# Projecting the convolution groups first and evacuating two tiles at once, in a one-core decoder trunk

## The chip, the cores and the metric

The kernel runs on one core of a Trainium2 chip. The metric is the device time of one execution in microseconds (us), the median over several runs. The kernel before takes 1127.89 us (three runs, 1125.96 to 1129.59).

The core's engines have names in the profile: PE is TensorE (matrix products), DVE is VectorE, ACT is ScalarE, POOL is GpSimd, SP is SyncE, which here only issues DMAs. Each engine works off its own queue of instructions in order. SBUF is the on-chip memory, PSUM the memory in which products are accumulated, in banks of 512 float32 columns.

## The reference, cut to what matters

One layer of a decoder on 256 prompt tokens and 8 x 4 sample tokens, 288 columns in all, in float32:

```python
h = rmsnorm(x, norm1_g)
proj = h @ w_in + b_in                      # 2048 -> 3072
a, gate, z = proj[:1024], proj[1024:2048], proj[2048:]
u = a * sigmoid(gate)
c = silu(layernorm(depthwise_causal_conv(concat(hist_conv, u), conv_w, conv_b)))   # 31 taps
d = window_mean(concat(hist_pool, z)) - z   # four groups of 256 channels, windows 2, 4, 8, 16
p = (d per group @ pool_w) * pool_scale
x = x + concat(c, p) @ w_out
f = square(relu(rmsnorm(x, norm2_g) @ w_ff1))   # 2048 -> 8192
x = x + f @ w_ff2
y = rmsnorm(x, norm_f)
```

The last 30 columns of `u` and the last 15 of `z` are returned too, as new states.

## The kernel before, in words

Activations lie with the channel on the partitions and the 288 tokens along the columns, one tile for 128 channels. Every float32 operand of a large product is split into a high and a low part, and a product is three matrix instructions: high x high, high x low, low x high (lines 233 to 235). Weights come in blocks of 1 MB by SP's DMAs (`load`, three buffers). `split` makes four half-parts of each pair of blocks: ACT copies out the high part (`whi`, line 213), and DVE or GpSimd subtracts it to get the low part (`wlo`, line 214). The table `SHARE` says how many of eight low parts go to GpSimd: 7 in a convolution group, 5 in a pooling group, 6 in the output projection's pooling half, none from there on. There are four buffers for high and four for low parts, so a group's parts are made while the group before is multiplied.

A group of products (`gemm`) fills two PSUM banks, m = 0 and 1, with 128 channels each; four banks (`acc`) let one group be read out while the next is multiplied.

The stages:

- Start: x is loaded in pieces, scaled and split (`hh`, `hl`), squares are summed in two chains, and `rsqrt_rows` makes the token's 1/rms, which later scales the projection's result as `rb`. `rsqrt_rows` uses small products (`pt`, line 182), a few tiny DVE operations (`st`), a diagonal (`dg`) and one more product (`pr`, line 196).
- Input projection: twelve groups of 96 products in the order of `SEQUENCE`. A `conv` group gives tile i of `a` and of `gate`: DVE reads both banks (`tg`, `ta`, lines 302 and 303), ACT applies the sigmoid, DVE makes `u` in `u_all` (line 308), and the convolution of that tile follows: for the prompt 31 taps on DVE, the first a `tensor_scalar` into PSUM (line 313), 29 more accumulating in PSUM and the last into `c` (line 316); for the samples four multiplications on GpSimd (`prd`) and a reduction on DVE (line 321). The convolution stands under `later()`, which gives it a low priority: the scheduler puts it where DVE has room. GpSimd sums the tiles `c` into `sum_c`. A `pool` group gives the two tiles of one pooling group. For each tile DVE reads the bank (`tz`, line 341), ACT adds the bias into `z_all`, GpSimd makes window sums by doubling (`s`, line 347: four additions for window 16, one for window 2), DVE makes `d` (line 351), its sample columns (line 354) and its first w - 1 columns (`e` and `d`, lines 358 and 359), ACT and DVE split it (`dh`, `dl`, line 362).
- Pool products: four groups of 12 products, g = 3, 2, 1, 0, scaled and split (`ph`, `pl`, line 380).
- LayerNorm of `c`: a product with ones gives the mean (`pmean`), DVE subtracts it (line 390), ACT squares, DVE adds up (`ssc`, line 397), `rsqrt_rows`, then scale, SiLU and split (`mh`, `ml`).
- Output projection: eight groups of 48 products over the pooling half, eight over the convolution half, each added to `xT`.
- MLP in four chunks of 2048: eight groups of 96 products up, eight down, with ReLU, square and split between.
- The last group of the last chunk is ordered with all of m = 0 first (`m_outer`), then the final RMSNorm.

The order of the instructions on each engine is made by a scheduler at build time, from the program's order, the priorities and its own estimate of durations. On the chip each queue is then strictly in order, with waits on the other engines' counters. The two state outputs have the lowest priority; SP's queue holds them among the weight loads.

## Time and profile before

| | |
|---|---|
| median of 3 runs | 1127.89 us |
| lowest, highest run | 1125.96, 1129.59 us |
| profiled execution: span from first to last instruction | 1125.9 us (the page gives no time around it) |
| PE busy | 1094.4 us, 97% |
| DVE busy | 677.1 us, 60% |
| ACT busy | 468.7 us, 42% |
| POOL busy | 188.8 us, 17% |
| data moved by DMA | 187 MB, 166 GB/s on the mean |

How to read it: busy times are sums over the span, so they hide stages with different limits. The page also shows the span in 40 slices, with each engine's busy tenths and PE's granted clock. Views of the trace give the same for any stretch (busy time and number of instructions of each engine, clock, DMA share), groups of instructions by line with their mean duration and the idle time before them, the waits by pair of engines, the chain of waits that ended last, and the instructions in order of time. Tile names stand as output<-inputs, buffer numbers left out.

### The profile page before, as it was taken

How to read it: one execution, taken by the hardware profiler on the slowest of the kernel's cores; microseconds unless marked ns; L12 is line 12 of the kernel's file. 1: busy time of each engine (PE TensorE's matmuls, PEld its weight loads, DVE VectorE, ACT ScalarE, POOL GpSimd, SP SyncE). 2: the span in 40 equal slices, each digit the busy share in tenths (PEclk: the TensorE clock that was granted, in tenths of full speed). 3: DMA queues.
4: the chain of work that ended last, by engine and by line, in shares of the span. 5: the costliest groups of instructions: out<-in, count | busy, mean ns of one | idle time of the engine just before them, and what ended most of it. 6: DMA issues, size and time to landing. Idle time of an engine off the chain costs nothing.

```text
span 1125.9 us, 19336 instructions
## 1 busy us (share of the span) xinstructions
PE 1094.4 (97%) x8190; PEld 1089.8 (97%) x8190; DVE 677.1 (60%) x983; ACT 468.7 (42%) x643; POOL 188.8 (17%) x149
## 2 busy tenths in 40 slices
PE   7998898999999999999999999999999999999995
PEld 7998898999999999999999999999999999999995
DVE  7999999788755544445555444455444445555554
ACT  6443345356544433334444333344433334444441
POOL 4789886612200000000000000000000000000000
PEclk9999998989999999999999999999999999999998
DMA  8554438534445444444445454444444454545432
GB/s 298 191 175 164 148 115 222 184 113 166 172 150 177 160 171 167 158 179 154 184 153 183 152 182 156 174 163 167 170 160 178 153 184 151 183 155 175 162 113 84
DMA packets 31910, 187.01 MB, mean 166 GB/s; under 512 B 3408, under 2 KB 7760, under 8 KB 10448
## 3 DMA queue, kind: packets, MB, share of 16 engines
q1 hardware_dynamic: 31824, 185.78, 47.0%
q8 instruction: 64, 1.05, 0.4%
q14 instruction: 22, 0.18, 0.0%
HBM read 181.49 MB, written 4.28 MB: 165 GB/s over the span
## 4 chain that ended last, share of the span: by engine, by line
PE 86%; DVE 9%; POOL 2%; issue 2%; DMA 1%; ACT 0%; SPq 0%; DVEq 0%; POOLq 0%
PE ac L233 29%; PE ac L234 28%; PE ac L235 28%; DVE pc L316 3%; DVE wlo L214 1%; POOL wlo L214 1%; DVE d L354 1%; DVE ssc L397 1%; DVE d L351 1%; DMA xT<-in_xT 1%; POOL s L347 0%; DVE d L359 0%; DVE z_all L283 0%; PE pt L182 0%; DVE xT L481 0%
## 5 line engine op out<-in xcount | busy, mean ns | idle before, releaser
L213 ACT CAST whi<-wr 128x1024 fp32r<-128x1024 f32 (+1 forms) x342 | 355.0, 1040 | 562.8 <-PE ac L234 543.6
L214 DVE TENSOR_TENSOR wlo<-wr,whi 128x1024 fp32r<-128x1024 f32 (+1 forms) x295 | 364.7, 1236 | 371.8 <-ACT whi L213 371.7
L233 PE MATMUL ac<-ah,whi 128*128 128x288 f32 x1024 | 302.7, 296 | 0.0
L233 PE MATMUL ac<-fh,whi 128*128 128x288 f32 x1024 | 302.4, 295 | 0.0
L234 PE MATMUL ac<-al,whi 128*128 128x288 f32 x1024 | 301.2, 294 | 0.0
L234 PE MATMUL ac<-fl,whi 128*128 128x288 f32 x1024 | 301.2, 294 | 0.0
L235 PE MATMUL ac<-fh,wlo 128*128 128x288 f32 x1024 | 299.3, 292 | 0.0
L235 PE MATMUL ac<-ah,wlo 128*128 128x288 f32 x1024 | 298.8, 292 | 0.0
L235 PEld LDWEIGHTS ac<-fh,wlo 128*128 128x128 f32 x1024 | 193.1, 189 | 0.0
L235 PEld LDWEIGHTS ac<-ah,wlo 128*128 128x128 f32 x1024 | 192.9, 188 | 0.0
L234 PEld LDWEIGHTS ac<-fl,whi 128*128 128x128 f32 x1024 | 192.7, 188 | 0.0
L234 PEld LDWEIGHTS ac<-al,whi 128*128 128x128 f32 x1024 | 192.4, 188 | 0.1
L233 PEld LDWEIGHTS ac<-ah,whi 128*128 128x128 f32 x1024 | 192.1, 188 | 0.1
L233 PEld LDWEIGHTS ac<-fh,whi 128*128 128x128 f32 x1024 | 192.0, 188 | 0.0
L233 PE MATMUL ac<-hh,whi 128*128 128x288 f32 x384 | 113.6, 301 | 7.7 <-DVE tg L302 6.6
L214 POOL TENSOR_TENSOR wlo<-wr,whi 128x1024 fp32r<-128x1024 f32 (+1 forms) x47 | 112.3, 2400 | 34.0 <-ACT whi L213 31.4
L234 PE MATMUL ac<-hl,whi 128*128 128x288 f32 x384 | 114.9, 301 | 3.0 <-DVE hl L246 2.9
L235 PE MATMUL ac<-hh,wlo 128*128 128x288 f32 x384 | 114.2, 301 | 1.5 <-DVE wlo L214 1.4
L316 DVE SCALAR_TENSOR_TENSOR pc<-u_all,vec,pc 128x256 f32<-128x256 f32 x232 | 100.1, 479 | 1.3
L233 PEld LDWEIGHTS ac<-hh,whi 128*128 128x128 f32 x384 | 73.3, 193 | 8.4 <-issue 7.0
L234 PEld LDWEIGHTS ac<-hl,whi 128*128 128x128 f32 x384 | 74.3, 194 | 4.1 <-DVE hl L246 4.1
L235 PEld LDWEIGHTS ac<-hh,wlo 128*128 128x128 f32 x384 | 74.1, 194 | 2.3 <-DVE wlo L214 2.2
(115 smaller groups left out, 875.5 us busy)
## 6 DMA issues: line engine op xcount, KB each, us to landing
wr<-in_w SPq DMA_DIRECT2D x167, 1024.0 KB, 4.9
xT<-in_xT SPq DMA_DIRECT2D x8, 288.0 KB, 5.7
wr<-in_w SPq DMA_DIRECT2D x8, 256.0 KB, 5.6
out_u_out<-u_all SPq DMA_DIRECT2D x1, 1208.0 KB, 8.6
out_yT<-xT SPq DMA_DIRECT2D x2, 576.0 KB, 2.9
u_all<-in_hist_c SPq DMA_DIRECT2D x8, 136.0 KB, 5.8
out_z_out<-z_all SPq DMA_DIRECT2D x1, 668.0 KB, 7.4
z_all<-in_hist_p SPq DMA_DIRECT2D x4, 152.0 KB, 4.0
```

What stands on the lines that cost most here:

```text
L213: nc.scalar.copy(hi[:, k : k + cut, :], src)
L214: eng.tensor_tensor(lo[:, k : k + cut, :], src, hi[:, k : k + cut, :].bitcast(F32), op=ALU.subtract)
L233: nc.tensor.matmul(b, wh, xh, start=k == 0, stop=False)
L234: nc.tensor.matmul(b, wh, xl, start=False, stop=False)
L235: nc.tensor.matmul(b, wl, xh, start=False, stop=k == n - 1)
L316: nc.vector.scalar_tensor_tensor(out=dst, in0=up[:, w : w + SEQ], scalar=cwv[:, w : w + 1], in1=pc, op0=ALU.mult, op1=ALU.add)
L351: nc.vector.scalar_tensor_tensor(out=d[:, w - 1 : SEQ], in0=s[:, PH + w - 1 : ZO], scalar=1.0 / w, in1=z[:, PH + w - 1 : ZO], op0=ALU.mult ...
L354: nc.vector.scalar_tensor_tensor(out=samples(d[:, SEQ:T], NS), in0=ss[:, :, PH:], scalar=1.0 / w, in1=zs[:, :, PH:], op0=ALU.mult, op1=ALU ...
L397: nc.vector.tensor_tensor(ssc, ssc, q, op=ALU.add)
```

## The change

`SEQUENCE` is now all eight convolution groups and then the four pooling groups, windows 16, 8, 4, 2; before, four convolution groups came first, then pooling and convolution groups took turns and a convolution group was last. The weight blocks in memory follow the same order. The two PSUM banks of a group are one tile of [128, 2, 512], and the activations' high and low parts of two neighbouring tiles are one tile of [128, 2, 2, 288]. With that, operations behind the products that were two instructions of 288 columns are one of 576, with `rb`, `mean`, `rl` or `r2` broadcast over the two halves (`both`): the reading of `a` and `gate` (`ag`), of `z` (`tz`), the window sums on GpSimd, `d` and its first columns, its split, LayerNorm's subtraction, squares, sums, scale and split, the additions to `xT` (except in the last chunk), and the MLP's ReLU, square and split. The sample columns of `d`, ACT's bias operations, the sigmoid, SiLU, and all that has a scalar for each channel stay one instruction for a tile. The first tap of each convolution moves from DVE to ACT. `sum_c` is summed over pairs of tiles on GpSimd, and `pmean` and LayerNorm's `pt` take both halves, so twice as many small products. Pools shrink accordingly: two buffers for most temporaries.

```diff
-SEQUENCE = [("conv", 0), ("conv", 1), ("conv", 2), ("conv", 3)]
-for _g in range(4):
-    SEQUENCE += [("pool", 3 - _g), ("conv", 4 + _g)]
 GROUPS = (3, 2, 1, 0)
+SEQUENCE = [("conv", _i) for _i in range(8)] + [("pool", _g) for _g in GROUPS]
...
-    acc = ctx.enter_context(tc.tile_pool(name="acc", bufs=4, space=PSUM))
+    acc = ctx.enter_context(tc.tile_pool(name="acc", bufs=2, space=PSUM))
...
+    def act2(name, **kw):
+        t = actp.tile([P, 2, 2, T], F32R, name=nm(name), **(kw or {"tag": "act"}))
+        return t[:, 0], t[:, 1]
...
+    def both(r):
+        return r[:, None, :T].to_broadcast([P, 2, T])
...
     def bank2():
-        return [acc.tile([P, 512], F32, name=nm("ac"), tag="ac") for _ in range(2)]
+        return acc.tile([P, 2, 512], F32, name=nm("ac"), tag="ac")
+
+    def halves(x2):
+        return [(x2[0][:, m, :], x2[1][:, m, :]) for m in range(2)]
...
-        ta, tg = tmp("ta"), tmp("tg")
-        nc.vector.tensor_tensor(tg, bk[1][:, :T], rb, op=ALU.mult)
-        nc.vector.tensor_tensor(ta, bk[0][:, :T], rb, op=ALU.mult)
+        ag = tmpp.tile([P, 2, T], F32, name=nm("ag"), tag="ag", bufs=2)
+        ta, tg = ag[:, 0, :], ag[:, 1, :]
+        nc.vector.tensor_tensor(ag, bk[:, :, :T], both(rb), op=ALU.mult)
...
-            nc.vector.tensor_scalar(pc, up[:, 0:SEQ], cwv[:, 0:1], v("conv_b", i), op0=ALU.mult, op1=ALU.add)
+            nc.scalar.activation(pc, up[:, 0:SEQ], AF.Identity, bias=v("conv_b", i), scale=cwv[:, 0:1])
...
-            if i == 0:
-                nc.gpsimd.tensor_copy(sum_c, c)
-            else:
-                nc.gpsimd.tensor_tensor(sum_c, sum_c, c, op=ALU.add)
+            if i == 3:
+                nc.gpsimd.tensor_tensor(sum_c, cs[0], cs[1], op=ALU.add)
+            elif i % 2 and i > 3:
+                nc.gpsimd.tensor_tensor(sum_c, sum_c, cs[i // 2], op=ALU.add)
...
+        tz = tmpp.tile([P, 2, T], F32, name=nm("tz"), tag="ag", bufs=2)
+        nc.vector.tensor_tensor(tz, bk[:, :, :T], both(rb), op=ALU.mult)
...
-                s2 = tmp("s", ZL, "s", 4)
-                nc.gpsimd.tensor_tensor(s2[:, 2 * w - 1 :], s[:, 2 * w - 1 :], s[:, w - 1 : ZL - w], op=ALU.add)
+            s2 = tmpp.tile([P, 2, ZL], F32, name=nm("s"), tag="s", bufs=2)
+            nc.gpsimd.tensor_tensor(s2[:, :, 2 * w - 1 :], s[:, :, 2 * w - 1 :], s[:, :, w - 1 : ZL - w], op=ALU.add)
...
-    nc.tensor.matmul(pmean[:, :T], ones, sum_c, start=True, stop=True)
+    for m in range(2):
+        nc.tensor.matmul(pmean[:, :T], ones, sum_c[:, m, :], start=m == 0, stop=m == 1)
...
-            for m in range(2):
-                t = tmp("t")
-                nc.vector.scalar_tensor_tensor(out=t, in0=bk[m][:, :T], scalar=0.0, in1=r2, op0=ALU.max, op1=ALU.mult)
+            t = tmpp.tile([P, 2, T], F32, name=nm("t"), tag="ag", bufs=2)
+            nc.vector.scalar_tensor_tensor(out=t, in0=bk[:, :, :T], scalar=0.0, in1=both(r2), op0=ALU.max, op1=ALU.mult)
...
                 xk = xT[:, k, :]
-                nc.vector.tensor_tensor(xk, xk, bk[m][:, :T], op=ALU.add)
                 if last:
+                    nc.vector.tensor_tensor(xk, xk, bk[:, m, :T], op=ALU.add)
...
+                elif m:
+                    x2 = xT[:, 2 * g : 2 * g + 2, :]
+                    nc.vector.tensor_tensor(x2, x2, bk[:, :, :T], op=ALU.add)
```

More of the change, by code (lines that the diff above doesn't have):

```diff
@@ L226, in gemm @@
         gets = ready.pop()
[L227 removed]
+        order = [(k, m) for k in range(n) for m in range(2)]
         if m_outer:
@@ new lines, in trunk_kernel @@
+    rl = rsqrt_rows([x[:, m, :] for x in (ssc, q) for m in range(2)], 1.0 / DC, AF.Silu)
+    mixc = []
+    for j, c in enumerate(cs):
+        n = tmpp.tile([P, 2, T], F32, name=nm("n"), tag="ag", bufs=2)
+        nc.vector.tensor_tensor(n, c, both(rl), op=ALU.mult)
+        for m in range(2):
+            i = 2 * j + m
+            nc.scalar.activation(n[:, m, :], n[:, m, :], AF.Silu, bias=v("ln_b", i), scale=v("ln_g", i))
+        mh, ml = act2("mx")
+        nc.scalar.copy(mh, n)
+        nc.vector.tensor_tensor(ml, n, f32(mh), op=ALU.subtract)
+        mixc += halves((mh, ml))
```

137 lines of the change are left out of this document (64 added, 73 removed).

## The prediction

> **What bounds the kernel now.** First the page: busy time, and the granted clock over 40 slices.
>
> ```profile
> PE 1094.4 (97%) x8190; PEld 1089.8 (97%) x8190; DVE 677.1 (60%) x983; ACT 468.7 (42%) x643; POOL 188.8 (17%) x149
> PE   7998898999999999999999999999999999999995
> DVE  7999999788755544445555444455444445555554
> PEclk9999998989999999999999999999999999999998
> ```
>
> TensorE is busy nearly always, but DVE is full in the first ten slices, and there PE has its gaps. So I cut the span into stages: from the DVE instruction that empties the second group's banks (44.00) to the one that empties the last convolution pair's (184.60), to the first output-projection product (192.76), to its convolution half (250.88), to the last MLP product (1111.40). The first row is a steady stretch, for the price of a product.
>
> ```profile
> 60.00:90.00 30.00, 30.00 (x229) 30.00 (x228) 30.00 (x67) 12.51 (x17) 25.16 (x20) 1.00 0.48 163
> ...
> 44.00:184.60 140.60, 130.78 (x972) 129.90 (x970) 138.91 (x284) 55.17 (x77) 120.89 (x82) 0.99 0.48 163
> 184.60:192.76 8.16, 7.67 (x37) 7.59 (x37) 8.01 (x20) 6.04 (x11) 7.09 (x6) 0.60 0.56 137
> 192.76:250.88 58.12, 56.08 (x403) 55.63 (x401) 47.16 (x93) 26.03 (x38) 23.56 (x11) 0.94 0.48 166
> 250.88:1111.40 860.52, 860.52 (x6544) 860.41 (x6543) 439.28 (x524) 354.48 (x471) 13.69 (x14) 1.00 0.46 162
> ```
>
> The columns are PE, PEld, DVE, ACT and POOL busy, then clock, DMA share and GB/s. A product costs 30/229 = 0.131 us, a projection group of 96 costs 12.6. From 250.88 on PE has no gap: nothing done to DVE or ACT there is worth anything. Between 44.00 and 184.60 lie ten groups, 126 us of products, in 140.6 us, and DVE works in 138.9 of them: DVE's queue is the bound there, POOL with 120.9 close behind. The waits say the same:
>
> ```profile
> PE ac L233 <- DVE tg L302: 9.8, 3, 3.6
> PE pt L182 <- DVE ssc L397: 2.0, 1, 2.0
> ...
> 185.00:190.00 5.00, 4.91 (x20) 4.83 (x21) 5.00 (x12) 4.61 (x9) 4.48 (x6) 0.50 0.31 113
> ```
>
> Three times PE waits for a bank that DVE has not read; once LayerNorm's statistics wait for `ssc`. After such a wait the clock is half (0.50 in the last row): 0.60 over the 8.16 us of the second stage makes 6.5 us at half clock, 0.94 over the third 7.0. A product then takes 0.24 us (20 in 4.91).
>
> **DVE's queue between the two evictions.** Its groups in that stretch, and rows for pitch (start to start is less than the duration: 24 taps in 9.48 us are 0.395 each, `tg` to `ta` is 0.37):
>
> ```profile
> L316 DVE SCALAR_TENSOR_TENSOR pc<-u_all,vec,pc 128x256 f32<-128x256 f32 x183 | 77.7, 478 | 0.7
> L354 DVE SCALAR_TENSOR_TENSOR d<-s,z_all 128x32 f32<-128x32 f32 x8 | 8.5, 1063 | 0.0
> L321 DVE TENSOR_REDUCE c<-prd 128x32 f32<-128x992 f32 x6 | 7.0, 1172 | 0.0
> L308 DVE SCALAR_TENSOR_TENSOR u_all<-ta,vec,tg 128x256 f32<-128x256 f32 x6 | 5.4, 899 | 0.2 <-ACT tg L304 0.2
> L351 DVE SCALAR_TENSOR_TENSOR d<-s,z_all 128x249 f32<-128x249 f32 x2 | 3.7, 1852 | 0.0
> L362 DVE TENSOR_TENSOR dl<-d,dh 128x288 fp32r<-128x288 f32 x8 | 3.6, 451 | 0.2
> L313 DVE TENSOR_SCALAR pc<-u_all,vec 128x256 f32<-128x256 f32 x6 | 3.2, 536 | 0.0
> L358 DVE TENSOR_TENSOR e<-s,rcnt 128x15 f32<-128x15 f32 x2 | 2.5, 1258 | 0.0
> L359 DVE TENSOR_TENSOR d<-e,z_all 128x3 f32<-128x3 f32 x2 | 2.1, 1072 | 0.0
> L351 DVE SCALAR_TENSOR_TENSOR d<-s,z_all 128x255 f32<-128x255 f32 x2 | 0.8, 408 | 0.0
> L358 DVE TENSOR_TENSOR e<-s,rcnt 128x7 f32<-128x7 f32 x2 | 0.3, 154 | 0.0
> ...
> 49.12 9.48 DVE L316 SCALAR_TENSOR_TENSOR pc<-u_all,vec,pc 128x256 f32<-128x256 f32 x24
> 58.52 0.44 DVE L302 TENSOR_TENSOR tg<-ac,rb 128x288 f32<-128x288 f32 x1
> 58.89 0.44 DVE L303 TENSOR_TENSOR ta<-ac,rb 128x288 f32<-128x288 f32 x1
> ```
>
> Note the pooling rows: 15 columns take 1258 ns, 7 columns 154; 249 columns 1852 ns, 255 columns 408. These operations read two SBUF operands and stand still while GpSimd works; taps, with one operand in PSUM, do not. All pooling elementwise work here is 40 operations and about 28 us, against 11 at the short durations.
>
> In the changed program's order of instructions, the stretch from the second eviction (`ag`, 576 columns) to the last (`tz` of pooling group 0) holds, against before:
> - taps 213 instead of 189, because convolutions are now all early: 24 x 0.395 = +9.5.
> - no first tap on DVE: 6 x 0.45 = -2.7. ACT takes them over; it is busy 55 of 140 us, so eight more of even 1 us lie beside other work. Were ACT full, they would delay the hi parts that PE needs next, 3 us for a quarter group.
> - 10 double evictions for 20 single ones. A double one is not in the trace; between 0.37 (all fixed) and 0.74 (nothing saved) I take 0.67: the rows of 7 and of 288 columns (154 and 451 ns) differ by 297 ns, so 288 more columns cost 0.30 on top of 0.37. 6.7 for 7.4: -0.7.
> - one `u_all` pair and one reduction more: +1.0, +1.1.
> - pooling: before four groups, 28 us less 3 of overlap = 25.4. Now three: three double `d` of 1.11, six sample parts (still one for each tile) of 1.06, three `e` of 0.43, three `d` heads of 0.76, two `dl` of 0.75, less overlap: 13.5. -11.9.
> - ten lo parts in both: 0.
>
> Sum -3.7: 136.9 us instead of 140.6. The unknown is the standing still: about 0.44 us for each pooling operation before. None of it would give 8 us more off; twice of it 8 us on. I keep 0.44, since GpSimd still computes 5 of 8 lo parts beside them. PE needs only 126 us, so it should no longer wait inside the stretch: a group's banks may be read one group late.
>
> **Handover to the output projection.** Before, 8.16 us. Now the last group is a pooling group, and its whole chain stands between its eviction and the fourth pool product. Queued on DVE from that eviction to the low part of its `d`: 13 taps 5.1, `tz` 0.67, two `dl` 1.3, four `px` low parts 1.7 (0.43 each, inside the 0.37 to 0.45 of the 288-column rows), `d` 0.6, sample parts, `e` and head 0.4 to 3 (as short as in the row of 255 columns, or standing still): 9.8 to 12.6, I take 10.3, the short end, as GpSimd has only one window sum left there. POOL's one sum and ACT's four bias operations stand beside the 6 us of taps and low parts queued ahead of `d`: 0, and about 1 to 2 us if GpSimd is late. Then 12 products at half clock, 2.9: 13.2 us. +5.0. `z_out` now stands in SP's queue behind that eviction, with weight block 3 of the output projection behind it, which is needed three blocks (19 us) later: 0. `u_out` (1.24 MB, 7.6 us at the stage's 163 GB/s) moves into group 8 in front of a block used two groups later: 0; if that cover went, at most those 7.6 us.
>
> **LayerNorm.** From the chain of waits, for the matrix products of the statistics:
>
> ```profile
> 222.42 0.50 PE pmean L385 x2
> ```
>
> The stage has 58.12 us for 384 products (50.3), `pmean`, `pt` and `pr`. Removed: the wait of 2.0 and the half clock after it. The last tap leaves DVE 18 us after the last eviction (the 10.3 above, eight more taps and `c` 3.6, four `px` 1.7, a lo part 1.4, with `xT` ahead 0.7), 5 after the output projection starts; the changed order asks for `pmean` 82 products (10.7) in, for `pt` 75 products later, for the first use of LayerNorm's result 193 products after `pr`. Needed then: 50.3 + two `pmean` 1.0 + 12 `pt` 1.9 (six take about 1.0 in the tail's row below) + `pr` 0.5 = 53.7. -4.4. Between `pmean` and `pt` lie 10 us for one ACT copy, four double subtractions, four squares and two sums, 6 to 11 us: this is late next if anything is; kept whole, the old wait costs +4.4.
>
> **Start.**
>
> ```profile
> 27.21 3.42 DVE L214 TENSOR_TENSOR wlo<-wr,whi 128x1024 fp32r<-128x1024 f32 x1
> ...
> 33.99 1.22 DVE L214 TENSOR_TENSOR wlo<-wr,whi 128x1024 fp32r<-128x1024 f32 x1
> ```
>
> The first, behind GpSimd's own lo part, took three times the second. In the new order this `wlo` comes ahead of the statistics, before GpSimd is released (its `memset` waits for `pt`): 1.2 instead of 3.42. Part of that PE had covered: -1.5, between -3 and +1 (`pt` now stands after 86 products, and PE waits for the last sum).
>
> **MLP.** Fewer, longer operations on DVE (439 of 861) and ACT (354): 0; the first use of a group's last two tiles lies 84 products (11 us) into the next phase.
>
> **Tail.** The two halves of the last group's banks are now one tile: in the new program the addition of tile 14 waits for the group's very last product, and `m_outer` no longer gives it 6 us of lead.
>
> ```profile
> 1111.62 0.46 DVE L466 TENSOR_TENSOR xT<-xT,ac 128x288 f32<-128x288 f32 x1 [4.88 <-PE ac L235]
> ...
> 1112.11 0.45 ACT q L472
> 1112.60 1.02 PE pt L182 x10
> ```
>
> One more addition and one square ahead of `pt`: +0.5.
>
> **Sum.** -1.5 - 3.7 + 5.0 - 4.4 + 0.5 = -4.1 us on a span of 1125.9. The page gives no time around the span; it lies 2.0 below the median 1127.9, so I forecast 1123.8.
>
> **Clock.** By the trace a wait of 2.0 us was followed by half clock. The Trainium skill (TensorE: Matmul & The Clock Gate, HAM oscillation) speaks of idle gaps above about 3.4 us. Were that so here, the 12 products would take 1.6 and the sum would be -5.4; the trace contradicts it, so half clock stays in.
>
> **Rivals.**
> - C, slower: standing still grows. GpSimd's window sums are now one instruction for two tiles:
>
> ```profile
> L347 POOL TENSOR_TENSOR s<-z_all 128x422 f32<-128x422 f32 x8 | 11.0, 1380 | 0.0
> L214 POOL TENSOR_TENSOR wlo<-wr,whi 128x1024 fp32r<-128x1024 f32 x45 | 109.2, 2435 | 29.7 <-ACT whi L213 27.1 <-DVE c L390 2.6
> ```
>
>   about 1.9 to 2.8 us at a stretch instead of 1.38, nearly a lo part. DVE's 24 pooling operations can each meet them, and now no conv group lies between the pooling groups. It decides from 4.1/24 = 0.17 us more for each; at 0.3 to 0.5 more it is +7 to +12: 1131 to 1136. For it: rows of 1.2 to 1.9 us above. Against it: half as many such operations. The Trainium skill (SBUF — State Buffer, Who interferes with whom) calls this port an exclusive lock held for the whole instruction, so longer instructions block longer; the trace's 3.42 beside a normal 1.2 agrees.
> - B, no difference: LayerNorm's wait returns, or the start's gain does not come: +1.5 to +4.4, 1126 to 1129.
> - D, more: the lower POOL share beside the pooling groups frees DVE; up to 8 less, and with it the handover's short end: 1116 to 1119. Against it: 0.44 is a mean over pooling groups that already had that share.
>
> **Chances.** Measurement tells 0.3% (3.4 us) from no change, so faster begins at 1124.5. Forecast 0.40 (its own range 1121 to 1127: 0.24 faster, 0.16 same), D 0.22 faster, B 0.20 (0.18 same, 0.02 slower), C 0.18 slower. Faster 0.46, same 0.34, slower 0.20. The range 1117 to 1132 cuts D's and C's outer ends.
>
> **What would show it.** Right: no PE wait between 44 and 165; one cluster of waits of 10 to 15 us around the pool products, ended by `tz`, `px` and `dx`; none at `pt`; first output-projection product near 191, its convolution half near 245. Wrong: PE waiting for `ag` in mid-stretch (C); a wait at `pmean` or `pt` (B); `d` rows of pooling all short (D).

## The result, and the profile after

The changed kernel takes 1140.26 us (median of four runs, 1139.98 to 1141.28), the kernel before in the same comparison 1126.93 (1125.07 to 1129.59): a ratio of 1.0121, interval 1.0105 to 1.0138. It is slower by 1.2%; forecast was 1123.8, slightly faster, and the measured time lies outside the range of 1117 to 1132. The traces differ by 12.7 us of span, 1138.6 against 1125.9.

From the page of the changed kernel, busy times and the granted clock in 40 slices:

```profile
PE 1106.6 (97%) x8204; PEld 1100.9 (97%) x8204; DVE 653.9 (57%) x827; ACT 468.1 (41%) x575; POOL 182.8 (16%) x134
DVE  7799999577754544444445444455444444554553
PEclk8999995999999999999999999999999999999997
```

DVE works 23 us less, as meant, and TensorE works 12 us more, on the same large products. The same stages as in the prediction, in the windows of the changed kernel (columns: PE, PEld, DVE, ACT, POOL busy, clock, DMA share, GB/s). The cuts are the second eviction, the last one, the first output-projection product, its convolution half, the last MLP product, the end:

```profile
45.14:183.47 138.33, 130.53 (x971) 129.72 (x969) 137.37 (x272) 58.03 (x78) 119.83 (x72) 0.97 0.51 169
183.47:197.70 14.23, 9.88 (x36) 8.90 (x37) 13.04 (x33) 6.21 (x13) 3.94 (x2) 0.50 0.59 123
197.70:254.54 56.84, 56.84 (x415) 56.52 (x415) 34.94 (x44) 28.62 (x38) 22.93 (x10) 0.95 0.43 148
254.54:1122.45 867.91, 867.91 (x6544) 867.73 (x6542) 429.87 (x417) 346.98 (x396) 13.36 (x14) 1.00 0.46 161
1122.45:1138.60 16.15, 3.26 (x16) 2.19 (x14) 7.97 (x17) 1.86 (x5) 0.00 (x0) 0.56 0.37 146
```

| stage | before | forecast | after | missed by |
|---|---|---|---|---|
| up to the second eviction | 44.00 | -1.5 | 45.14 (+1.1) | 2.6 |
| DVE's queue, second to last eviction | 140.60 | -3.7 | 138.33 (-2.3) | 1.4 |
| handover to the output projection | 8.16 | +5.0 | 14.23 (+6.1) | 1.1 |
| pooling half, LayerNorm | 58.12 | -4.4 | 56.84 (-1.3) | 3.1 |
| convolution half and MLP | 860.52 | 0 | 867.91 (+7.4) | 7.4 |
| tail | 14.50 | +0.5 | 16.15 (+1.6) | 1.1 |

The signs of four stages are as forecast. The largest loss is where nothing was forecast: in the MLP, where TensorE never waits, at full clock, with the same count of 6544 in the row. The other five stages miss by 9.3 us together, all to the slow side. One up-projection phase (768 products) in the trace of before:

```profile
505.55:606.46 100.91, 100.91 (x771) 100.91 (x769) 51.24 (x63) 42.94 (x60) 0.00 (x0) 1.00 0.47 167
```

and the same phase in the trace of after:

```profile
510.89:612.75 101.86, 101.86 (x770) 101.86 (x769) 50.56 (x47) 42.34 (x46) 0.00 (x0) 1.00 0.47 165
```

100.91/768 is 0.1314 us for a product, 101.86/768 is 0.1326. In this phase the products start 0.0012 us further apart; over the 6528 large products of the stage it is 0.0011 us on the mean, which makes the 7.4 us. (The counts in the rows include small products and records at both edges of a window.) I call this distance the pitch.

What the stretches before it wait for, from the waits of PE between 40 and 260 us, changed kernel:

```profile
PE ac L237 <- ACT dx L371: 5.3, 2, 5.1
PE ac L239 <- DVE wlo L218: 3.6, 2, 2.9
PE ac L237 <- DVE px L389: 2.7, 1, 2.7
PE ac L238 <- DVE dx L372: 0.5, 1, 0.5
```

No wait for an eviction (`ag`) is left, and none at `pmean` or `pt`; but for 0.7 us at 163.8, all stand around the pool products. That picture was forecast. The cut at the last eviction (183.47) runs through this cluster: the 2.9 us and 4.2 of the 5.1 lie ahead of it, in the row of DVE's queue.

### The profile page after: what moved, and what is told of

Same layout as the page of the kernel before. It is cut to its first block, busy times and chain, and to the rows that moved or that the text cites. A ratio compares the mean times of both kernels' runs of the same rounds, so it can differ in the third digit from the quotient of the medians.

```text
span 1138.6 us, 19071 instructions
## 1 busy us (share of the span) xinstructions
PE 1106.6 (97%) x8204; PEld 1100.9 (97%) x8204; DVE 653.9 (57%) x827; ACT 468.1 (41%) x575; POOL 182.8 (16%) x134
## 4 chain that ended last, share of the span: by engine, by line
PE 82%; DVE 14%; POOL 1%; issue 1%; ACT 1%; DMA 1%; SPq 0%; DVEq 0%; POOLq 0%
PE ac L237 27%; PE ac L238 27%; PE ac L239 27%; DVE pc L327 7%; DVE wlo L218 1%; DVE u_all L317 1%; DVE c L332 1%; DVE hx L256 1%; DMA xT<-in_xT 1%; POOL wlo L218 1%; PE pt L186 1%; DVE d L359 0%; DVE ag L312 0%; DVE xT L499 0%; POOL s L356 0%
## 5 line engine op out<-in xcount | busy, mean ns | idle before, releaser
L237 PE MATMUL ac<-fx,whi 128*128 128x288 f32 x1024 | 303.6, 296 | 0.0
L237 PE MATMUL ac<-ax,whi 128*128 128x288 f32 x1024 | 303.5, 296 | 0.0
L239 PE MATMUL ac<-fx,wlo 128*128 128x288 f32 x1024 | 301.8, 295 | 0.0
L239 PE MATMUL ac<-ax,wlo 128*128 128x288 f32 x1024 | 301.6, 294 | 0.0
L238 PE MATMUL ac<-fx,whi 128*128 128x288 f32 x1024 | 301.3, 294 | 0.0
L238 PE MATMUL ac<-ax,whi 128*128 128x288 f32 x1024 | 301.3, 294 | 0.0
L239 PEld LDWEIGHTS ac<-ax,wlo 128*128 128x128 f32 x1024 | 192.5, 188 | 0.0
L238 PEld LDWEIGHTS ac<-ax,whi 128*128 128x128 f32 x1024 | 192.3, 188 | 0.1
L237 PEld LDWEIGHTS ac<-fx,whi 128*128 128x128 f32 x1024 | 192.3, 188 | 0.0
L237 PEld LDWEIGHTS ac<-ax,whi 128*128 128x128 f32 x1024 | 192.2, 188 | 0.1
L239 PEld LDWEIGHTS ac<-fx,wlo 128*128 128x128 f32 x1024 | 192.2, 188 | 0.0
L238 PEld LDWEIGHTS ac<-fx,whi 128*128 128x128 f32 x1024 | 191.9, 187 | 0.0
L237 PE MATMUL ac<-hx,whi 128*128 128x288 f32 x384 | 116.1, 302 | 1.4 <-ACT whi L217 1.4
L238 PE MATMUL ac<-hx,whi 128*128 128x288 f32 x384 | 115.0, 299 | 0.4 <-DVE hx L256 0.4
L237 PEld LDWEIGHTS ac<-hx,whi 128*128 128x128 f32 x384 | 73.8, 192 | 1.8 <-ACT whi L217 1.8
L238 PEld LDWEIGHTS ac<-hx,whi 128*128 128x128 f32 x384 | 73.7, 192 | 1.0 <-DVE hx L256 0.9
```

Source lines behind the costliest of these rows:

```text
L237: nc.tensor.matmul(b, wh, xh, start=k == 0, stop=False)
L238: nc.tensor.matmul(b, wh, xl, start=False, stop=False)
L239: nc.tensor.matmul(b, wl, xh, start=False, stop=k == n - 1)
```

## The experiments

The theories at the start, for the MLP: (A) the place in SBUF of the high and low parts that TensorE streams decides the pitch, since the change put a pair's four parts in one tile as high 0, high 1, low 0, low 1; (B) the wide operations of DVE and ACT disturb the products; (C) the weights' buffers moved by 2304 bytes, since the pools ahead of them shrank. For the rest: is it the order of the groups, or the pairing?

From here on the stage with the MLP is cut at the start of its last product, and so it takes 860.41 us before and 867.78 in the changed kernel. The stages in front of it move between executions of one program: the second trace of the kernel before (experiment 12) has 142.48 us in DVE's queue, 7.52 in the handover and 55.06 in the pooling half, where the first has 140.60, 8.16 and 58.12.

**1. Parts interleaved again, in the changed kernel.**

```diff
-        return t[:, 0], t[:, 1]
+        return t[:, :, 0], t[:, :, 1]
```

> The changed kernel, but each pair's tile of high and low parts is laid out high 0, low 0, high 1, low 1 (as neighbours, as the kernel before has them) instead of high 0, high 1, low 0, low 1; nothing else differs, and TensorE's order is the same. Theory A (where the parts lie decides the time of a product): the product's pitch in the MLP goes from 0.1327 back to 0.1315 us, the stretch from the convolution half of the output projection to the last MLP product from 867.9 to about 860.5 us, the time to 1131 to 1134. Theory B (the wide operations of DVE and ACT disturb the products): pitch stays at 0.1327, 1140. Theory C (the weights' buffers have moved by 2304 bytes): also 1140.

Measured: 1136.20 us, ratio to before 1.0077 (1.0059 to 1.0094), 4.1 us less than the changed kernel. The window from the convolution half to the last MLP product:

```profile
254.35:1118.94 864.59, 864.59 (x6544) 864.48 (x6542) 429.89 (x417) 347.68 (x396) 13.34 (x14) 1.00 0.47 161
```

3.2 of 7.4 us come back; DVE and ACT do the same wide operations, and the weights lie where they lay. So the place acts (against B and C as the only cause), but this placing is not as good as that of before: every phase without small products in it is at 0.1322.

**2. The paired placing alone, in the kernel before.** All operations stay single.

```diff
     def act(name, **kw):
-        return actp.tile([P, T], F32R, name=nm(name), **(kw or {"tag": "act"}))
+        tag, bufs = kw.get("tag", "act"), kw.get("bufs", 40) // 4
+        t, n = quad.get(tag, (None, 4))
+        if n == 4:
+            t, n = actp.tile([P, 2, 2, T], F32R, name=nm(name), tag=tag, bufs=bufs), 0
+        quad[tag] = (t, n + 1)
+        return t[:, n % 2, n // 2, :]
```

> The kernel before, every operation still one tile at a time, but the high and low parts of two neighbouring tiles share a tile laid out high 0, high 1, low 0, low 1. Theory A (layout): pitch in the MLP 0.1327 instead of 0.1315, time 1127 plus 7 to 9, 1134 to 1136. Theories B (wide operations) and C (place of the weights' buffers): no change, 1127, since neither is touched.

Measured: 1135.79 us, ratio 1.0079 (1.0062 to 1.0097).

```profile
249.21:1117.07 867.86, 867.86 (x6541) 867.75 (x6542) 438.71 (x525) 354.27 (x473) 14.07 (x14) 1.00 0.46 161
```

867.86 us, the changed kernel's 867.78 to a tenth, without one wide operation (DVE's count is 525, not 417). This settles the largest term as far as the edit goes: the new placing alone brings the whole 7.4 us, and B and C fall as its cause. It goes with the placing and not with what runs in front: the four kernels with this placing (the changed one, experiments 2, 4 and 11) have 0.1328 already in the input projection, from its third group on, and the kernel before has 0.1322 there. How the placing acts is not shown, and experiment 10 loses 5.7 us in this stage with no place in it changed.

**3. The new order of the groups alone, in the kernel before.**

```diff
-SEQUENCE = [("conv", 0), ("conv", 1), ("conv", 2), ("conv", 3)]
-for _g in range(4):
-    SEQUENCE += [("pool", 3 - _g), ("conv", 4 + _g)]
+SEQUENCE = [("conv", _i) for _i in range(8)] + [("pool", 3 - _g) for _g in range(4)]
```

> The kernel before with the new order of the groups alone (eight convolution groups, then pooling windows 16, 8, 4, 2), all operations single. By the prediction's steps the DVE queue between the second and the last eviction gets 24 taps, 2 first taps, a u_all pair and a reduction more (+12.5) and a quarter of the pooling work less (-6.4): +6; the handover +5 to +8, LayerNorm's wait -4: 1134 to 1138. If the new order is harmless and the pairing is what costs: 1127 to 1129.

Measured: 1140.03 us, ratio 1.0122 (1.0099 to 1.0144): by itself as slow as the whole change, and slower than the 1134 to 1138 expected. Its windows, cut at the second eviction, the last eviction and the convolution half:

```profile
44.23:186.74 142.51, 130.51 (x972) 129.17 (x970) 142.28 (x284) 53.93 (x71) 121.20 (x83) 0.97 0.49 164
186.74:263.27 76.53, 65.89 (x437) 63.60 (x437) 61.86 (x118) 36.22 (x63) 28.51 (x16) 0.85 0.42 133
263.27:1123.71 860.44, 860.44 (x6543) 860.33 (x6542) 436.50 (x516) 351.01 (x462) 13.38 (x14) 1.00 0.47 162
```

The handover and the pooling half together take 76.53 us instead of 8.16 + 58.12 = 66.28: +10.2. DVE's queue takes +1.9, no more than it moves between executions, and the MLP is untouched. The late pooling chains are the price of the order; the pairing then wins part of it back.

**4. The changed kernel with the old order of the groups.** The edit of experiment 3, backwards.

> The changed kernel with the order of groups of before (pooling and convolution groups taking turns, a convolution group last); pairs, ACT's first tap and layout stay. If the new order is what costs outside the MLP: the handover is back at about 8 us and the stretch before it is shorter by the pairs' saving (2.7 for the first taps, 0.7 for the evictions, some 10 for pooling), so 1140 less 6 less up to 9: 1125 to 1134, with the MLP still 7.4 longer. If the pairing itself costs at the front (double operations hold banks and the port longer): 1140 or above.

Measured: 1134.79 us, ratio 1.0068 (1.0053 to 1.0083).

```profile
44.76:180.98 136.22, 131.13 (x971) 130.24 (x969) 135.27 (x264) 56.92 (x79) 118.78 (x69) 0.99 0.51 168
180.98:193.34 12.36, 8.22 (x36) 7.64 (x36) 11.56 (x27) 7.30 (x13) 6.59 (x6) 0.72 0.73 186
```

Without the new order the pairs gain 4.4 us in DVE's queue (136.22 against 140.60). But the handover, with a convolution group last as before, is 12.36 us and not about 8 as expected. The waits of PE between 120 and 260 us (that for GpSimd's low part stands at 163, in DVE's queue):

```profile
PE ac L239 <- DVE px L391: 3.3, 2, 2.7
PE ac L241 <- POOL wlo L220: 3.2, 2, 2.5
PE ac L239 <- DVE ag L314: 2.7, 1, 2.7
```

In the program a pair's two banks are one tile now and come free together, so a product can wait for both to be read; no run isolates what that costs here. The MLP's stage is at 867.77 us again. The order costs 5.5 us beside the pairs (1140.26 less 1134.79), the pairs in front of the MLP about nothing in sum.

**5. Interleaved, and shifted by 128 bytes.** (Its text calls the first experiment the second.) From here on the question is which rule of place sets the pitch.

```diff
+    padp = ctx.enter_context(tc.tile_pool(name="padp", bufs=1))
+    padt = padp.tile([P, 32], F32, name="padt")
     actp = ctx.enter_context(tc.tile_pool(name="actp", bufs=10))
```

> The changed kernel with the parts interleaved (high 0, low 0, high 1, low 1) as in the second experiment, and everything behind the weights' buffers moved up by 128 bytes, so that each high part begins at a multiple of 256 bytes and each low part 128 bytes behind one; before the shift it is the other way round. The weights' parts begin 128 bytes behind a multiple of 256 in both. Theory A1 (what counts is where each part begins, modulo 256 bytes): pitch in the MLP 0.1311 instead of 0.1322 us, the stretch of 864.6 us becomes 857 to 858, the time 1128 to 1130. Theory A2 (what counts is only how far the low part lies from the high one): pitch 0.1322, time 1136.

Measured: 1134.62 us (1129.01 to 1135.32), ratio 1.0065 (1.0041 to 1.0090); the stage 864.55 us, 0.1322. A1, the place modulo 256 bytes, fails as a rule that fixes the pitch by itself.

**6. The kernel before, low part first.** One tile of 2 x 288 for a channel tile; `act` hands out its second half, then its first.

> The kernel before, each channel tile's two parts in one tile of 2 x 288, the low part first, so that every high part begins at a multiple of 256 bytes and every low part 128 behind one; in the kernel before that holds for most of the tiles, the pitch is 0.1311 for these and 0.1322 for the others. Nothing else is changed. Theory A1: all at 0.1311, 0.0005 us for some 7000 products, 3 to 4 us less: 1123 to 1124. Theory A2 (distance only; the low part now lies below the high one everywhere): pitch 0.1322 everywhere, 1131.

Measured: 1133.95 us, ratio 1.0069 (1.0053 to 1.0086).

```profile
250.82:1118.94 868.12, 868.12 (x6541) 868.01 (x6542) 438.81 (x525) 355.87 (x473) 14.15 (x14) 1.00 0.46 161
250.82:256.80 5.98, 5.98 (x25) 5.98 (x26) 4.66 (x12) 4.99 (x12) 0.00 (x0) 0.50 0.48 175
```

Not 3 us less but 7.7 more. Of these about 2.7 are not the pitch: the stage begins at half clock, behind a wait of 3.0 us for `mh`, and its first 25 products take 0.24 us each. The other 5.0 are: the down-projections run at 0.1322 and the up-projections from the second chunk on at 0.1325, where A1 had 0.1311. A1 falls again.

**7. Four placings in one kernel.** Each part has 32 spare columns; the down-projection's operands of each chunk take another choice.

```diff
+        t = actp.tile([P, 2, 2, T + 32], F32R, name=nm(name), tag="act")
+        h, l = ((0, 0), (32, 32), (0, 32), (32, 0))[lay]
+        return t[:, :, 0, h : h + T], t[:, :, 1, l : l + T]
```

> The changed kernel with room between the parts of the activations, so that both places can be chosen, another choice for the up-projection's results in each of the four MLP chunks (begin of the high, begin of the low part modulo 256 bytes): 128 and 128, 0 and 0, 128 and 0, 0 and 128. Some buffers are single for the room, so its total time says nothing; read are the four phases of 768 down-projection products. Theory A1: 0.1322 in the third, 0.1311 in the fourth, and from the pitches measured so far (two kinds of neighbours) about 0.1348 in the first and 0.1316 in the second. Theory A2: all four alike.

The four down-projection phases of 768 products:

```profile
409.77:510.89 101.12, 101.12 (x771) 101.12 (x769) 46.02 (x41) 35.00 (x34) 0.00 (x0) 1.00 0.48 167
612.54:714.94 102.40, 102.40 (x770) 102.40 (x769) 46.03 (x41) 34.99 (x34) 0.00 (x0) 1.00 0.47 165
816.59:918.14 101.55, 101.55 (x770) 101.55 (x769) 46.02 (x41) 35.05 (x34) 0.00 (x0) 1.00 0.48 166
1019.79:1121.30 101.51, 101.51 (x770) 101.48 (x768) 48.12 (x58) 42.54 (x59) 0.00 (x0) 1.00 0.36 126
```

0.1317, 0.1333, 0.1322, 0.1322. The first two have the same distance from high to low part (1280 bytes) and differ by 1.3%: A2, distance alone, falls too as a rule that fixes the pitch by itself. Phases whose tiles are all placed alike differ, in these traces, by steps of about 0.00056 us.

**8. The weights' buffers shifted too.** The 128 bytes of experiment 5 lie ahead of the weights' split buffers instead.

> As the interleaved and shifted kernel, but the 128 bytes lie ahead of the weights' split buffers, so that these begin at a multiple of 256 bytes too (before: 128 behind). Theory A1 with the place of the activations alone: pitch 0.1311 still. Theory A3 (the place relative to the weights counts, since the next product's weights are loaded while this one streams): as high odd, low even before, 0.1322.

Measured: 1136.96 us in one run; the stage 864.59 us, all phases at 0.1322. A1 is against it; A3 forecast the value, but as 0.1322 came with the weights at either place (experiments 5 and 8), the run does not tell A3 from no influence of the weights.

**9. Place and order of the two tiles of a pair, by chunk.** On the kernel of experiment 5:

```diff
-        order = [(k, m) for k in range(n) for m in range(2)]
+        order = [(k ^ swap, m) for k in range(n) for m in range(2)]
...
+            fh, fl = act2("fx", first=ch % 2)
...
+            gemm(bk, fx, m_outer=last and g == 7, swap=ch // 2)
```

> The changed kernel with interleaved parts, shifted by 128 bytes as in the fifth experiment; read are the four phases of 768 down-projection products, which differ in two things: in the second and fourth chunk the low part lies below the high one instead of above, in the third and fourth the products take the two tiles of a pair in the other order, so that from tile to tile the place always falls by 2304 bytes, as for most tiles of the kernel before. Theory A4 (the direction from tile to tile decides): third or fourth phase at 0.1311, first and second at 0.1322. Theory A5 (neither): all four at 0.1322, and why the kernel before reaches 0.1311 stays open.

Measured: 1131.87 us in one run. From the first down-projection on, phase by phase:

```profile
405.28:505.97 100.69, 100.69 (x770) 100.69 (x769) 46.01 (x41) 34.85 (x34) 0.00 (x0) 1.00 0.48 168
505.97:606.67 100.70, 100.70 (x771) 100.70 (x770) 50.58 (x47) 42.43 (x46) 0.00 (x0) 1.00 0.47 168
606.67:708.25 101.58, 101.58 (x771) 101.58 (x769) 46.02 (x41) 34.96 (x34) 0.00 (x0) 1.00 0.47 166
708.25:809.79 101.54, 101.54 (x770) 101.54 (x769) 50.62 (x47) 42.46 (x46) 0.00 (x0) 1.00 0.48 167
809.79:911.34 101.55, 101.55 (x770) 101.55 (x769) 46.05 (x41) 34.91 (x34) 0.00 (x0) 1.00 0.47 166
```

The down-projections of the third and fourth chunk, in swapped order, stay at 0.1322 (the last row is the third's): A4 falls. So does A5, as the first is at 0.1311. And something neither theory had: the second and the fourth row are up-projections of different chunks, with the same operands at the same places in the same order, and run at 0.1311 and 0.1322. So the place is not all; something else, such as what ran before, counts too. Between the two lies the down-projection whose low parts lie below the high ones.

**10. The first tap on ACT alone, in the kernel before.**

```diff
-            nc.vector.tensor_scalar(pc, up[:, 0:SEQ], cwv[:, 0:1], v("conv_b", i), op0=ALU.mult, op1=ALU.add)
+            nc.scalar.activation(pc, up[:, 0:SEQ], AF.Identity, bias=v("conv_b", i), scale=cwv[:, 0:1])
```

> The kernel before with one part of the change alone: the first tap of each convolution on ACT. By the step of the prediction (six of the first taps lie in the stretch that DVE's queue bounds, 0.45 us each): 2.7 us less between the second and the last eviction, 1124. Rival (ACT comes late, so the taps behind it or the high parts wait): 1127 to 1129.

Measured: 1132.29 us, ratio 1.0057 (1.0044 to 1.0071), slower. In DVE's queue the saving does not arrive: the six first taps (3.2 us) are gone and DVE is as busy as before, 138.86 us against 138.91. The stretch, with 141.74 us here and 140.30 in the second trace, is not clear of the 140.60 and 142.48 of the kernel before (first row: between the second and the last eviction; second row: convolution half and MLP):

```profile
44.06:185.80 141.74, 131.85 (x972) 130.98 (x970) 138.86 (x280) 58.57 (x83) 119.70 (x82) 0.98 0.48 161
248.25:1114.40 866.15, 866.15 (x6544) 866.04 (x6543) 439.15 (x524) 354.54 (x469) 13.48 (x14) 1.00 0.46 161
```

Of DVE's groups in that stretch, the two that grew most, and its low parts of the weights:

```profile
L214 DVE TENSOR_TENSOR wlo<-wr,whi 128x1024 fp32r<-128x1024 f32 x10 | 14.2, 1423 | 1.5 <-ACT whi L213 1.5
L354 DVE SCALAR_TENSOR_TENSOR d<-s,z_all 128x32 f32<-128x32 f32 x8 | 11.5, 1440 | 0.0
...
L362 DVE TENSOR_TENSOR dl<-d,dh 128x288 fp32r<-128x288 f32 x8 | 5.8, 727 | 0.1
```

The sample parts were at 1063 ns and the low parts of `d` at 451: 5.2 us more of standing still than before, for the same 16 operations. Others stood still less, so that all 40 pooling operations together took 30.2 us where they had taken 28.6. Two more taps fall into the stretch, and DVE stood idle 1.5 us for ACT's high parts, 0.5 before: the rival has its part. What makes the kernel slower is the other stage: convolution half and MLP take 866.15 us, at 0.1325, though all its products have the operands, order and banks of the kernel before.

**11. The last group's results in two tiles again, in the changed kernel.**

```diff
+            if last and g == 7:
+                b2 = (bk, bank2())
+                gemm(b2, fx, m_outer=True)
```

> The changed kernel, but the two halves of the last group's results lie in two tiles, so that the addition of the first half need not wait for the group's last product. By the prediction's step the tail loses one addition and one square, 0.5 us; by the traces (16.3 us behind the last product instead of 14.6) 1.0 to 1.7 us. Time 1138.5 to 1139.8.

Measured: 1137.50 us in one run, below the 1138.5 to 1139.8 expected. Its tail:

```profile
1120.63:1135.70 15.07, 2.72 (x17) 1.72 (x15) 7.16 (x15) 1.18 (x3) 0.00 (x0) 0.57 0.40 157
```

From the same cut, the start of the last product, the changed kernel has 16.28 us and others with its tail (experiments 1, 4, 8, 9) 15.74: 0.7 to 1.2 us for the lost lead. The MLP is again at 867.8. What else is gained is not the edit's: the pooling half, for one, took 54.61 us instead of 56.84, at full clock.

**12 to 14. Second traces: the kernel before; experiment 10; experiment 5.**

> The kernel before, unchanged, for a second trace. Theory S (the products' pitch falls into one of a few levels and stays there, and which one can differ between executions): its MLP phases may show other levels than 0.1314 and 0.1319. Theory F (each program has its fixed pitch): again 0.1314 for the up-projections, 0.1314 and 0.1319 by turns for the down-projections, 860.4 us in all.

> The kernel before with the first tap on ACT, a second trace; its products of the MLP read and write the same places in the same order as those of the kernel before, and yet ran at 0.1325 instead of 0.1314 to 0.1319. Theory S: another level is possible, down to 860.4 us for the stage. Theory F: again 0.1325 and 866.1 us.

> The interleaved and shifted kernel, a second trace; its four timed runs were 1129.0, 1134.2, 1135.0 and 1135.3. Theory S: 0.1322 (864.6 us for the stage) or, as in two phases of the ninth experiment, 0.1311 (857 us). Theory F: 0.1322.

The first ran in 1126.32 us, the second in 1129.96, the third in 1137.03. The stage from the convolution half to the last MLP product takes 860.41 us in the first and 866.14 in the second. In the third, the convolution half (384 products) and an up-projection (768) take:

```profile
255.50:305.85 50.35, 50.35 (x387) 50.35 (x385) 38.64 (x38) 27.57 (x44) 12.36 (x13) 1.00 0.47 168
510.38:611.92 101.54, 101.54 (x770) 101.54 (x769) 50.62 (x47) 42.47 (x46) 0.00 (x0) 1.00 0.47 167
```

Two of the three repeat their stage to a tenth of a microsecond, which speaks for F. But the third has its convolution half at 0.1311 and the MLP at 0.1322, where its first trace had 0.1322 in both: the same program at two levels. In the third the pitch turned within the first MLP phase: 0.1311 ahead of the small products of the RMSNorm, 0.1322 behind them. So experiment 5's 0.1322 was not the only level of its program, and what experiments 5 and 7 to 9 rule out is a rule of place that fixes the pitch by itself.

**15. A combination.** The changed kernel with the old order, the parts interleaved and shifted, and two tiles for the last group.

> The changed kernel with the old order of the groups, the parts interleaved and shifted, and the last group's results in two tiles. From the fourth experiment's 1134.8: less 3.2 for the pitch at 0.1322 or less 10.4 at 0.1311, less 1 for the tail: 1130.5 or 1123.5, by the level that holds.

Measured: 1130.88 us (1128.86 to 1134.45), ratio 1.0043 (1.0028 to 1.0058), with 0.1322 in the whole MLP (864.55 us): the higher of the two forecasts. It is 9 us better than the changed kernel and does not beat the kernel before.

**16 and 17. One more small product at the start of TensorE's queue**, in the kernel before and in that of experiment 10.

```diff
-    rcnt = const.tile([P, PH], F32, name="rcnt")
+    rcnt = const.tile([P, PH + 1], F32, name="rcnt")
+    nc.vector.memset(rcnt[:, PH : PH + 1], 1.0)
...
+    nc.tensor.matmul(warm[0:1, 0:TB], rcnt[:TB, PH : PH + 1], ident, start=True, stop=True)
```

> The kernel before with one more small product in TensorE's warm-up, which needs two waits, so that TensorE's queue holds an odd number of instructions more ahead of everything else; all places of operands and the order of the 8112 large products are those of the kernel before. Theory Q (the pitch depends on where TensorE's instructions lie in its queue, odd or even; the kernel with the first tap on ACT has one wait fewer there): the MLP's pitch becomes 0.1325, its stage 866.1 us, the time 1132. Theory L (the level is caught by chance of timing at the start of the MLP): may be either; 860.4 and 1126 if nothing of the timing there matters.

> The kernel before with the first tap on ACT and the same additional small product: theory Q: the pitch returns from 0.1325 to 0.1314 to 0.1319, the stage from 866.1 to 860.4 us, the time from 1131 to about 1125. Otherwise 866.1 and 1131.

The first took 1126.71 us, ratio 1.0006 (0.9996 to 1.0016):

```profile
250.92:1111.33 860.41, 860.41 (x6543) 860.30 (x6542) 439.14 (x524) 354.45 (x471) 13.69 (x14) 1.00 0.46 162
```

The second took 1131.37 us, ratio 1.0043 (1.0029 to 1.0058), with 866.15 us in this stage.

Q falls: both keep their pitch. 860.4 is the time of four traces now (before twice, order only, this), 866.1 that of three.

**18. Disturbing the stream**, in the kernel of experiment 10.

```diff
     for ch in range(DFF // FCH):
         fx = []
+        for _ in range((0, 1, 3, 8)[ch]):
+            br = ms("br")
+            cols = (0, 128, 8, 1)[ch]
+            nc.tensor.matmul(br[:, 0:cols], ones, ones[:, 0:cols], start=True, stop=True)
```

> The kernel before with the first tap on ACT (MLP at 0.1325 in all three traces), and small products that nothing reads put between the large ones: one of 128 columns at the start of the MLP's second chunk, three of 8 columns at the start of the third, eight of one column at the start of the fourth. The places of all operands of the large products stay. Theory H (the products run in one of several rhythms, which hold until something disturbs them, and which the front part happened to set): from the second, third or fourth chunk on the pitch changes, to 0.1314 to 0.1319 or to another level, and stays there to the next disturbance. Theory G (the rhythm is set anew all the time by something that this program differs in from the kernel before): 0.1325 in all chunks, with only the small products' own time on top.

Measured: 1131.34 us in one run; the stage takes 863.23 us with the small products in it. The first two down-projections, the first with the small product that ends it:

```profile
405.02:506.48 101.46, 101.46 (x772) 101.46 (x771) 46.87 (x51) 35.02 (x37) 0.00 (x0) 1.00 0.47 167
607.48:708.38 100.90, 100.90 (x770) 100.90 (x769) 46.74 (x51) 34.93 (x36) 0.00 (x0) 1.00 0.47 167
```

Such a phase took 101.76 us in experiment 10. From start to start the pitch is 0.1319 and 0.1314, the levels of the kernel before, and that from the first chunk on, ahead of all disturbances. Those left it as it was. So neither H nor G is borne out as put: the level was another than in the three sibling traces from the MLP's beginning, and stayed.

## Why the prediction was wrong, step by step

**MLP: 0.** This is the step that failed. The prediction took the products' pitch as given ("a product costs 30/229 = 0.131 us") and asked only whether DVE and ACT keep up; they do. But the change also moved TensorE's operands, and experiment 2 shows that the new placing alone brings 7.4 us, 0.0011 us for each product. Four programs with the paired placing (the changed kernel, experiments 2, 4, 11) have 867.8 to 867.9 us. The prediction costed the new tiles as instructions only, and gave no bound for a product that is no longer the same product to the memory. Had this term been known, the forecast would have been 1131, near the upper end of its range; the 9.3 us of the other misses would still have put the measured time outside it.

What rule of place acts, and whether the place acts by itself or through the level that the products fall into, stays open: with the operands, order and banks of the kernel before, experiment 10's stage takes 866.15 us, 1.6 less than the changed kernel's. Steps of 256 bytes, distance, order and place in the queue were tried and fell; the same operands ran at two levels in one trace (experiment 9), and the same program in two traces (experiment 14). That a level is caught at the RMSNorm's small products and then kept would fit experiments 14 and 18, but is only argued. The Trainium skill (TensorE: Matmul & The Clock Gate, Wait — 56ns, not 53.3ns?) speaks of a fixed cost of about 2.5 ns for each matmul beside one column a cycle; here the cost beside the columns is not fixed, since equal products took 131.1 to 133.3 ns.

**LayerNorm: -4.4, measured -1.3.** The wait at `pt` went, as forecast. The step that failed is "the half clock after it" as something that goes with the wait. The statistics products of the changed kernel in order of time, two of its windows, and then the whole stage in experiment 12 (the kernel before again) and in experiment 11 (the changed kernel with another tail):

```profile
220.19 2.12 PE L186 MATMUL pt<-ones,q 128*96 128x1 f32 x24
222.30:227.00 4.70, 4.70 (x26) 4.70 (x26) 1.43 (x8) 2.69 (x4) 1.67 (x1) 0.64 0.67 223
197.70:201.00 3.30, 3.30 (x20) 3.30 (x20) 2.22 (x4) 1.59 (x3) 0.00 (x0) 0.73 0.00 0
194.01:249.07 55.06, 53.02 (x402) 52.57 (x401) 47.35 (x94) 25.91 (x38) 23.67 (x12) 1.00 0.53 177
198.24:252.85 54.61, 54.61 (x414) 54.29 (x415) 35.28 (x45) 28.03 (x38) 22.94 (x10) 1.00 0.43 154
```

PE does not wait, but for 2.1 us it has only 24 tiny products, and half clock follows here all the same: 26 products in 4.70 us instead of 3.5, and at the stage's start 20 in 3.30 instead of 2.6, left over from the handover's waits. With 0.6 us for the pitch, 53.7 becomes about 56.2; 56.84 was measured. But neither the wait nor the tiny products decide it: experiment 12 has the same wait of 2.0 us for `ssc` and experiment 11 the same 24 products, both with the clock at 1.00 in the whole stage. With half clock in both traces the change gains 1.3 us here (58.12 to 56.84), without it in both 0.45 (55.06 to 54.61). So 3.1 us of the 58.12 that the prediction started from belong to that one execution; what decides it is not shown. The Trainium skill (TensorE: Matmul & The Clock Gate, HAM oscillation) names idle gaps above about 3.4 us; here half clock came, where it came, behind 2.1 us of little work and behind waits of 2.0 us, and in experiment 4 behind waits of 2.7 us.

**Start: -1.5, measured +1.1.** The mechanism came (the first `wlo` of 1.22 us ahead of the statistics), the gain did not: other operations stood still, such as the `hx` pairs at 10.04 and 21.36, for 2.97 and 3.02 us where others of their kind take 0.94. But kernels with the same order at the start reached the second eviction between 43.16 (experiment 9) and 46.90 us (experiment 8), so a step of this size cannot be judged there.

**DVE's queue: -3.7, measured -2.3.** 213 taps start in the stretch, as counted, and double evictions are 0.67 us apart as estimated. Mis-sized was the standing still, that of `u_all` most. By groups, between these evictions:

```profile
L317 DVE SCALAR_TENSOR_TENSOR u_all<-ag,vec 128x256 f32<-128x256 f32 x7 | 7.4, 1063 | 0.0
...
L317 DVE SCALAR_TENSOR_TENSOR u_all<-ag,vec 128x32 f32<-128x32 f32 x7 | 3.8, 546 | 0.0
L372 DVE TENSOR_TENSOR dx<-d,dx 128x576 fp32r<-128x576 f32 x2 | 3.2, 1621 | 0.0
L359 DVE SCALAR_TENSOR_TENSOR d<-s,z_all 128x482 f32<-128x482 f32 x1 | 2.8, 2847 | 0.9 <-POOL s L356 0.9
...
L368 DVE TENSOR_TENSOR e<-s,rcnt 128x30 f32<-128x30 f32 x1 | 2.4, 2386 | 0.0
L364 DVE SCALAR_TENSOR_TENSOR d<-s,z_all 128x32 f32<-128x32 f32 x6 | 2.2, 411 | 0.0
```

`u_all` took 11.2 us where it had taken 6.8, +4.4 for the +1.0 counted: 1063 ns each for 256 columns (899 before), 546 for 32 columns (241 before). `d` and `e` of window 16 and the `dx` of window 8 (2.50 us at 177.17) took far more than the 1.11, 0.43 and 0.75 that were put in, the sample parts less than the 1.06; all pooling operations together 15.8 us busy where 14.8 were counted. Against that, the taps' busy time grew by 7.5 us where 9.5 were counted. That DVE stands still was kept at 0.44 us an operation; it is not a price for an operation: the 32-column sample part took 1063 ns before, 411 here and 1440 in experiment 10.

**Handover: +5.0, measured +6.1.** Right in mechanism: the last pooling chain and half clock. The low part of the last `d` was done 11.4 us behind the last eviction (10.3 forecast), and the output projection began 2.9 us later (2.9 forecast), at clock 0.50. The cluster of waits that was to show it is there, 11.4 us around the pool products, but most of it stands ahead of this stage.

**Tail: +0.5, measured +1.6.** Right in mechanism, mis-sized: experiment 11 gives 0.7 to 1.2 us back for the lead alone. The kernel before has 14.6 us in its first trace and 15.1 in its second, from the start of the last product, so the rest is not clear of that.

**The rivals.** The sign was that of C, the mechanism was not: PE waited for no `ag` in mid-stretch, and DVE's stretch was shorter than before. B's wait did not come back. The order, forecast as part of the handover, is what costs most in front: experiment 3 has +10.2 us there with single operations, experiment 4 5.5 with pairs. Three figures of the prediction do not follow from its own terms: its sum puts the first output-projection product at 192.6 and the convolution half at 246.3, not 191 and 245 (197.70 and 254.54 were measured), B's terms make 1125 to 1128, and the handover's queue adds up to at most 12.4.

## What to carry to other kernels

When a change alters the tiles that the bound engine reads, its own instructions may no longer take the same time, even if their number, shape and order are the same; compare the start-to-start distance of two equal phases before looking for waits. A saving in a queue whose operations stand still for another engine may not be worth its duration: experiment 10 took 3.2 us of taps away and the stretch was not clearly shorter. A wait's price that is read from one trace may hold a half clock that the next execution does not have; take a second trace of the kernel before. And single-part experiments can mislead when a whole stage far behind moves too: read each by its stages, not by its total.

## What the runs showed of the hardware

- Products of 288 columns, with PE never idle and the clock at 1.00, start 0.1311 to 0.1333 us apart; phases whose tiles are all placed alike lie on steps of about 0.00056 us. Inside a phase of the MLP without small products, groups of 96 repeat to 0.0001 us.
- The value goes with the place of the streamed operand in SBUF (experiments 1 and 2, and 4 and 11 with the place of 2; 6 and 7 fit that), and can differ for the same operands (experiments 9, 14, and 10 against 18).
- Half clock came behind 2.1 us of tiny products and behind a wait of 2.0 us, but not in every trace: with the same products (experiment 11) and the same wait (experiment 12) the clock stayed at 1.00.
